# Keys stored by residue mod 4 for dilated attention, and each query part transposed once with the exchanged half copied by VectorE

## The chip, the cores and the metric

The kernel runs on one core of one Trainium2 chip. The metric is device time in microseconds (us) of one execution, as the median of the runs; smaller is better. The profile shows one execution of the same program, with its engines: TensorE (PE, and PEld for its weight loads), VectorE (DVE), ScalarE (ACT), GpSimd (POOL) and SyncE (SP). In this kernel SP issues all the DMA transfers.

## The reference

One inference step of one decoder layer, on a prompt of 2048 rows of 1024 numbers and on a sample of 8 x 8 tokens against a cache. A normed input goes through one input projection, whose columns are split among two mixers and their gates. The part that matters here is mixer A on the prompt: attention of 8 heads of width 64, in three branches, (window, dilation) = (128, 1), (512, 4) and (2048, 16), whose outputs are weighted by their softmax denominators.

```python
DILATED = ((128, 1), (512, 4), (2048, 16))

def mixer_layer(x, pos, attend, s0, ...):
    h = rmsnorm(x, norm_w)
    z = h @ w_in
    q, k, v, qb, kb, vb, g_lr, gate_a, gate_b = jnp.split(z, split_points(), axis=-1)
    q = rope(rmsnorm(heads(q, H_A), q_norm_w), pos)
    k = rope(rmsnorm(heads(k, H_A), k_norm_w), pos)
    o_a = attend(q, k, v)                       # mixer A
    o_b, s_fin = gla_chunked(qb, kb, vb, log_a, s0)   # mixer B, gated linear attention
    mixed = concatenate([o_a * silu(gate_a), rmsnorm(o_b, gla_norm_w) * silu(gate_b)])
    return x + mixed @ w_out, k, v, s_fin

def dilated_branch_prompt(q, k, v, window, dil):
    # rows are sorted by their residue mod dil; in each residue, blocks of 128 queries
    # see their own block of 128 keys and the one ahead of it
    qr, kk, vv = by_residue(q), with_prev(by_residue(k)), with_prev(by_residue(v))
    valid = (dist >= 0) & (dist < window // dil + 1) & (key_m >= 0)
    s = jnp.where(valid, einsum(qr, kk) * hd ** -0.5, -inf)
    m = s.max(-1); p = exp(s - m); den = p.sum(-1)
    return einsum(p, vv) / den, m + log(den)

def dilated_mixture(results):                   # over the three branches
    return einsum(softmax(lses), outs)
```

So branch 1 works on adjacent rows, branch 2 on rows 4 apart, branch 3 on rows 16 apart.

## The kernel before

Numbers go through TensorE in fp16, as a high part and a low part that together carry the fp32 value; a product of two such numbers is made of products of parts that are summed in PSUM.

**Projections.** `project` (L1052) multiplies tiles of 128 rows by one block of the input weights (v, q, k, then qkb, g, vb, gb), 24 products of 512 columns for a block of 512. `first(m)` runs v, q and k for the four tiles of group m (512 rows): at m=0 block by block, later tile by tile. Behind each, `qk_store` norms and rotates q and k, splits them into parts (ScalarE the high part, VectorE the low one) and stores them in device memory: `kp_d` holds for each row and head the key's high and low part (2 x 64), `qp_d` holds the query's high part twice and its low part twice (4 x 64). The values' parts go to `vp_d`.

**Keys and queries on chip.** A transposing DMA turns 128 rows by 128 columns into a block of 128 partitions by 128 columns. `keys(m, a)` does so for row tile a of group m, all 8 heads, into `kk`: partitions 0 to 63 hold the high part, 64 to 127 the low part, and the columns hold rows in their order, 512 for each of two groups. `queries(m, pp)` does the same for 4 heads (pp is the half of the heads) into `qq`, with 8 blocks: for each head one of (high, high) and one of (low, low). A score is then two products over 128 partitions, with a query block as weights and the keys as moving columns: high x (high, low), and low x (high, low).

**Attention.** `attend` works on 2 heads (branches 1 and 2) or 4 heads (branch 3), in three stages. `qk`: the score products (PE, L408); for each head one VectorE instruction that adds the mask and finds the maximum (L416), and one exponential on ScalarE (L419). `tr`: transposes of the result on PE (L426), which are split into parts (L388 to L393). `pv`: products with the values (L441); `added` (L452 to L458) then sums the two halves. `unit(m, pp, br, x)` makes two calls of attend, for branch 1 on block x of 128 queries of group m, for branch 2 on the queries of residue x mod 4. It loads its own value tile `v` (L825, for branch 2 by rows 4 apart) and stores its output to `o_d` (L840). In branch 2 both operands are read on chip in steps of 4 columns:

```python
qs = slice(x, 512, 4)
of = lambda k: k[:, :, qs] if nb == 2 else k[:, m % 2, qs]
```

With nb = 2 a block sees 256 keys, of two groups in branch 2; at m=0 branch 2 has one block of 128 keys. `kk` holds two groups; where the newer one stands in the first of the two places, the halves of keys, values and mask are in swapped order (`swap`).

`branch3(r)` handles residue r mod 16 for all 8 heads: transposing DMAs of 128 rows 16 apart (L879) give `T_q` (16 blocks, 512 KB) and `T_k` (8 blocks, 256 KB); a value tile; two calls of attend; a store of `o` (L896). The tiles `T_q`, `T_k`, `v` and `o` of branch 3 have two buffers each.

**What sets the order.** Calls of attend stand in a queue `work`. `pipeline()` runs item n's `qk`, item n-2's `pv` and item n-1's `tr` in turns, and runs an item's `pre` (transposes and value load) ahead of its `qk` and already behind the `qk` of the item before. `pump()` advances it a step at a time: during `first(m)` of group 1 on, 3 x 0.62 steps behind each group of three products, and later by `weave`, which mixes lists of work by their shares. A scheduler then places the instructions on each engine by a simulated timeline, and the engine works through its list in that order. DMAs are all in SP's list; beside what a transfer waits for by its data, it waits until the eighth transfer ahead of it on its semaphore ring has landed. The sample's score dots (`dot`: GpSimd L921, VectorE L922), loads of the cache and projections of mixer B run beside the attention.

Of the kernel before, what the change touches and what calls it, by code (L numbers as in the profile page):

```python
# [7 lines left out]
F32 = mybir.dt.float32  # L8
# [10 lines left out]
P = 128  # L19
# [33 lines left out]
def tile_hymba(ctx: ExitStack, tc: tile.TileContext, A: dict):  # L53
# [28 lines left out]
    qp_d = dram.tile([S, 4 * NH * HD], F16, name="qp_d")  # L82
# [23 lines left out]
    ident8 = cp.tile([P, P], F32, name="ident8")  # L106
    DVE.tensor_scalar(ident8[:], ident[:], 0.125, None, ALU.mult)

    ident64 = cp.tile([P, 64], F32, name="ident64")
    for r0 in (0, 64):  # L110
        DVE.tensor_copy(ident64[r0 : r0 + 64], ident8[r0 : r0 + 64, r0 : r0 + 64])
# [235 lines left out]
    with ExitStack() as c1:  # L347
# [18 lines left out]
        xp = right(c_first, "xp", 2)  # L366
        sp = c_att.enter_context(tc.tile_pool(name="sp", bufs=3))
# [376 lines left out]
        def qk_store(nm_, o, n, t, rows):  # L744
# [7 lines left out]
            c = 2 if nm_ == "q" else 1  # L752
            p_ = xp.tile([P, NH, 2, c, HD], F16, name=f"{nm_}p_{t}", tag=f"{nm_}p", bufs=1)
            src = o.rearrange("p (h d) -> p h d", h=NH)
            h, l = p_[:, :, 0], p_[:, :, 1]
            if c == 1:
                h, l = h[:, :, 0], l[:, :, 0]
                ACT.activation(h, src, AF.Copy, scale=scl["k"][:])
                DVE.scalar_tensor_tensor(l, src, scl["k"][:], h, ALU.mult, ALU.subtract)
            else:  # L760
                src = src.unsqueeze(2).to_broadcast([P, NH, 2, HD])
# [3 lines left out]
                (qp_d if c == 2 else kp_d)[rows, :], p_[:].rearrange("p h a c d -> p (h a c d)")  # L765
# [20 lines left out]
        def keys(m, a):  # L786

            r0 = 512 * m + P * a
            SP.dma_start_transpose(kk[:, :, m % 2, P * a : P * a + P], kp_d[r0 : r0 + P, :])

        def queries(m, pp):

            q = qs_[m, pp] = ap_.tile([P, 8, 512], F16, name=f"qq_{m}_{pp}", tag="qq")
            for a in range(4):
                r0 = 512 * m + P * a
                SP.dma_start_transpose(
                    q[:, :, P * a : P * a + P], qp_d[r0 : r0 + P, 1024 * pp : 1024 * pp + 1024]
                )

        def unit(m, pp, br, x):  # L800
            oc = slice(pp * 264, (pp + 1) * 264)
            if br == 1:
                n = 4 * m + x
                key, prev, dct, nb = n, n - 1, v1, (2 if n else 1)
                sel = lambda ap: ap[128 * n : 128 * n + 128]
            else:
                key, prev, dct, nb = (x, m), (x, m - 1), v2, (2 if m else 1)
                sel = lambda ap: ap[512 * m : 512 * m + 512].rearrange("(i c) f -> c i f", c=4)[x]
# [4 lines left out]
            def pre():  # L813
# [11 lines left out]
                SP.dma_start(vt[:], sel(vp_d[:, pp * 512 : (pp + 1) * 512]))  # L825
# [17 lines left out]
            for a in range(2):  # L843

                def scores(i, a=a):
                    if br == 2:
                        qs = slice(x, 512, 4)
                        of = lambda k: k[:, :, qs] if nb == 2 else k[:, m % 2, qs]
                    else:
                        qs = slice(P * x, P * x + P)  # L850
# [967 lines left out]
```

## Time and profile before

| | |
|---|---|
| runs (us) | 1457.05, 1461.98, 1464.38; median 1461.98 |
| profiled execution: span (us) | 1458.2 |
| mean granted TensorE clock over the span | 0.962 |
| instructions | 26397 |

The page gives for the profiled execution its span, from the first to the last instruction, and no separate time; the span lies 3.8 us under the median of the runs.

Where the stages lie, with the busy time of each engine in them (us, from the stretches of the trace):

| stretch (us) | what runs | PE | DVE | ACT | POOL | DMA share |
|---|---|---|---|---|---|---|
| 75 to 243 | v, q, k of the first groups, attention of m=0 | 141.17 of 168 | 120.60 | 104.64 | 60.01 | 0.69 |
| 243 to 655 | m=1 to 3, beside projections | 380.18 of 412 | 308.08 | 292.22 | 244.56 | 0.81 |
| 655 to 845 | branch 3 | 151.34 of 190 | 101.02 | 123.53 | 69.16 | 0.85 |
| 845 to 1458 | mixer B, gates, output, sample | 562.39 of 613 | 404.74 | 291.45 | 237.69 | 0.56 |

How to read the rows of the profile further down. A group's row has line, engine, operation, output<-inputs with partitions x elements, a count, and busy time with the mean of one in ns. A row of the timeline has start (us), length (us), engine, line, operation and a count of neighbours put together; SPq is the DMA queue's issue on SP. A row of DMA issues ends with the median time from issue to landing. A stretch's row has its length, the busy time of PE, PEld, DVE, ACT and POOL (with counts), the granted clock, the DMA share and GB/s. Busy time of an engine that nothing waits for costs nothing.

### The profile page before, as it was taken

What the parts mean: (1) busy time and instruction counts of PE and PEld (TensorE: products, weight loads), DVE (VectorE), ACT (ScalarE), POOL (GpSimd) and SP (SyncE); (2) the same over time, 40 slices, a digit from 0 to 9 for tenths busy, and PEclk for the clock granted to TensorE, in tenths of its full rate; (3) what the DMA queues carried; (4) which work ended last, traced back from release to release, by engine and by line L of the source; (5) the groups of instructions that cost most, each with busy time, mean ns of one, the idle gap of its engine ahead of it and who ended that gap; (6) DMA issues with size and microseconds to landing.
All of it is one profiled execution on the core that took longest, in us unless ns stands there. A gap on an engine that the chain in (4) does not pass through costs nothing.

```text
span 1458.2 us, 26397 instructions
## 1 busy us (share of the span) xinstructions
PE 1279.5 (88%) x8878; PEld 736.1 (50%) x8878; DVE 977.7 (67%) x2397; ACT 861.7 (59%) x2295; POOL 615.9 (42%) x564
## 2 busy tenths in 40 slices
PE   3787898989999889995869999889899969999997
PEld 1333455555555455664556655656655534444342
DVE  6576687788778946655655446799998697674222
ACT  7545687667668775765658744777787552222120
POOL 0042232656677644654351357555573345431000
PEclk9998999999999999997899999999999989999998
DMA  9867668577986799879998453333235759999661
GB/s 281 258 178 181 174 182 216 138 233 227 214 215 179 230 239 263 310 197 237 273 226 198 139 147 94 109 123 115 89 103 181 270 180 315 347 308 314 227 203 56
DMA packets 287962, 297.93 MB, mean 204 GB/s; under 512 B 158978, under 2 KB 189779, under 8 KB 287827
## 3 DMA queue, kind: packets, MB, share of 16 engines
q1 hardware_dynamic: 287826, 296.25, 69.6%
q8 instruction: 70, 1.15, 0.3%
q14 instruction: 66, 0.53, 0.1%
HBM read 183.19 MB, written 79.43 MB: 180 GB/s over the span
## 4 chain that ended last, share of the span: by engine, by line
PE 30%; DVE 20%; DMA 20%; ACT 12%; issue 7%; POOL 5%; SPq 5%; DVEq 0%; POOLq 0%; ACTq 0%
PE Y L1418 10%; DMA o_d<-o 5%; PE acc_gb L1052 4%; ACT p L419 3%; DMA k<-in_cache_k_win 3%; PE OS L1667 3%; DMA x<-in_x_prompt 2%; POOL pr L921 2%; DVE p L416 2%; PE s L408 2%; PE acc_qkb L1052 2%; DVE qbd L221 2%; PE t L426 1%; DVE sck L922 1%; PE acc_q L1052 1%
## 5 line engine op out<-in xcount | busy, mean ns | idle before, releaser
L1052 PEld LDWEIGHTS <-hr 128*128 128x128 f16 x1824 | 178.0, 100 | 149.7 <-issue 28.4
L921 POOL TENSOR_TENSOR pr<-k,qb 128x512 f32<-128x512 f32 x128 | 173.8, 1358 | 180.9 <-DVE sck L922 87.0
L419 ACT ACTIVATE p<-p,o 128x256 f32<-128x256 f32 (+1 forms) x384 | 173.0, 453 | 91.5 <-DVE o L416 84.6
L1052 PEld LDWEIGHTS <-hl 128*128 128x128 f16 x1248 | 122.9, 101 | 148.7 <-issue 33.6
L1418 PE MATMUL Y<-w_o,mh 128*128 128x512 f16 x768 | 180.9, 382 | 6.8 <-DVE xr L1425 4.4
L416 DVE CUSTOM_DVE_ANT_0 p<-s,m3w,scl_s 128x256 f32<-128x256 f32 (+1 forms) x384 | 143.7, 419 | 57.6 <-DMA o_d<-o 39.1
L393 POOL TENSOR_TENSOR pt<-p,pt 128x512 f16<-128x512 f32 (+1 forms) x80 | 94.8, 1186 | 158.0 <-ACT pt L392 121.8
L441 PE MATMUL O<-v,pt 128*128 128x128 f16 x1200 | 115.2, 223 | 33.6 <-POOL pt L393 15.3
L426 PE MATMUL t<-ident,p 128*128 128x128 f32 x600 | 116.2, 289 | 30.1 <-ACT p L419 26.8
L922 DVE TENSOR_REDUCE sck<-pr 128x8 f32<-128x512 f32 x128 | 87.0, 680 | 79.7 <-POOL pr L921 79.6
L1418 PEld LDWEIGHTS <-mh 128*128 128x128 f16 x768 | 72.0, 98 | 100.1 <-issue 27.0
L441 PEld LDWEIGHTS <-pt 128*128 128x128 f16 x1200 | 84.7, 100 | 68.3 <-POOL pt L393 21.5
L1052 PE MATMUL acc_v<-w_v,hl 128*128 128x512 f16 x384 | 99.8, 399 | 19.6 <-ACT zs_k L648 9.1
L408 PE MATMUL s<-kk,qq 128*128 128x256 f16 (+1 forms) x512 | 107.9, 324 | 9.6 <-DVE o L416 8.0
L1052 PE MATMUL acc_g<-w_g,hr 128*128 128x272 f16 (+1 forms) x768 | 103.9, 284 | 1.0 <-ACT vbs L722 1.0
L426 PEld LDWEIGHTS t<-ident,p 128*128 128x128 f32 x600 | 73.0, 146 | 58.4 <-ACT p L419 42.4
L1052 PE MATMUL acc_q<-w_q,hl 128*128 128x512 f16 x384 | 96.3, 388 | 1.6 <-ACT zs_q L648 1.4
L1052 PE MATMUL acc_k<-w_k,hl 128*128 128x512 f16 x384 | 95.1, 382 | 2.5 <-ACT zs_k L648 1.7
L1052 PE MATMUL acc_vb<-w_vb,hr 128*128 128x512 f16 x384 | 90.8, 384 | 5.8 <-DVE so_g L622 5.8
L1052 PE MATMUL acc_gb<-w_gb,hr 128*128 128x512 f16 x384 | 90.3, 391 | 5.8 <-DVE so_gb L622 5.8
L1384 ACT ACTIVATE mh<-tm 128x1024 f16<-128x1024 f16 x32 | 31.9, 1020 | 104.0 <-PE tm L1383 104.0
L210 ACT ACTIVATE E<-D_e 128x256 f32<-128x256 f32 (+1 forms) x168 | 67.9, 412 | 32.0 <-DVE ks L217 20.7
(523 smaller groups left out, 2590.8 us busy)
## 6 DMA issues: line engine op xcount, KB each, us to landing
k<-in_cache_k_win SPq DMA_DIRECT2D x104, 256.0 KB, 4.8
sv<-in_cache_v_win SPq DMA_DIRECT2D x104, 256.0 KB, 5.9
hr<-h_d SPq DMA_DIRECT2D x44, 512.0 KB, 4.7
qb<-q_d SPq DMA_DIRECT2D x64, 256.0 KB, 4.9
oc<-o_d SPq DMA_DIRECT2D x48, 264.0 KB, 5.7
o_d<-o SPq DMA_DIRECT2D x64, 132.0 KB, 4.1
x<-in_x_prompt SPq DMA_DIRECT2D x16, 512.0 KB, 5.6
h_d<-hl SPq DMA_DIRECT2D x16, 512.0 KB, 4.9
```

The costliest lines, as they stand in the source:

```text
L210: ACT.activation(E[rows, i, :n], D[rows, half], AF.Exp, scale=1.0 / 16.0)
L393: POOL.tensor_tensor(l, f, h, ALU.subtract)
L408: PE.matmul(s_ps[:, i * w : (i + 1) * w], q, k, start=(n == 0), stop=(n == len(prods) - 1),)
L416: DVE.tensor_tensor_reduce(s[:, sl], s_ps[:, sl], mask, neg, BIG, ALU.add, ALU.min, nmf(i))
L419: ACT.activation(s[:, sl], s[:, sl], AF.Exp, bias=nmf(i), scale=-1.0, accum_out=denf(i))
L426: PE.transpose(p_ps[:, i * P : (i + 1) * P], t["s"][:, i * P : (i + 1) * P], ident[:])
L441: PE.matmul(o_, t["pt"][:, c, (i * nb + b) * P : (i * nb + b + 1) * P], vf(i, b), start=(n == 0), stop=(n == 2 * nb - 1),)
L921: POOL.tensor_tensor(pr[:], kt, qt, ALU.mult)
L922: DVE.tensor_reduce(out, pr[:].rearrange("p (u k d) -> p u k d", u=2, k=4), AX.X, ALU.add)
L1052: PE.matmul(z, a_[:, k, :], w[:, p_, k, cols], start=(k == 0 and i == 0), stop=(k == KT - 1 and i == 2),)
L1418: PE.matmul(Y[:], a_[:, k, :], w_[:, part, k, :512], start=(i == 0), stop=(i == len(prods) - 1),)
L1667: PE.matmul(OS[32 * x : 32 * x + 32, 0:256], ps(x), vs_[bb][:, 256 * u : 256 * u + 256], start=(i == 0), stop=(i == 13),)
```

## The change

- **Keys.** `keys(m, c)` now transposes the 128 rows of group m with residue c mod 4, and `kk` has the form (head, residue, group mod 2, 128). Branch 2 reads the keys of a residue as adjacent columns, 128 or 256. Branch 1 reads the block x as four runs of 32 adjacent columns, one of each residue; its keys are then in another order, so its value tile is loaded with the same order of rows (`sel_k`), and it has a mask of its own, `m3c`, made from `m3w` by one GpSimd instruction.
- **Queries.** `qp_d` holds each part once. `queries` transposes 4 blocks of (high, low) in place of 8, and `exchanged` has VectorE copy them with the halves of the partitions swapped: (low, high). The two products of a score are then (high, low) x (high, low) and (low, high) x (high, low). Branch 2 still reads the queries in steps of 4. In branch 3 `T_q` is transposed with 8 blocks, and its other 8 are copied the same way.
- **The rest.** `ident8` is gone (ident64 is scaled straight from ident), and the two masks lie in a pool of their own.

```diff
@@ -79,7 +79,7 @@
     kp_d = dram.tile([S, 2 * NH * HD], F16, name="kp_d")
-    qp_d = dram.tile([S, 4 * NH * HD], F16, name="qp_d")
+    qp_d = dram.tile([S, 2 * NH * HD], F16, name="qp_d")
     vp_d = dram.tile([S, 2 * NH * HD], F16, name="vp_d")
@@ -103,12 +103,11 @@
     nw = const("nw", [P, KT], A["norm_w"][0].rearrange("(k p) -> p k", p=P))
-    ident8 = cp.tile([P, P], F32, name="ident8")
-    DVE.tensor_scalar(ident8[:], ident[:], 0.125, None, ALU.mult)
-
     ident64 = cp.tile([P, 64], F32, name="ident64")
     for r0 in (0, 64):
-        DVE.tensor_copy(ident64[r0 : r0 + 64], ident8[r0 : r0 + 64, r0 : r0 + 64])
+        DVE.tensor_scalar(
+            ident64[r0 : r0 + 64], ident[r0 : r0 + 64, r0 : r0 + 64], 0.125, None, ALU.mult
+        )
     ones = cp.tile([P, 1], F32, name="ones")
@@ -364,6 +363,7 @@
         xp = right(c_first, "xp", 2)
+        at1 = c_att.enter_context(tc.tile_pool(name="at1", bufs=1))
         sp = c_att.enter_context(tc.tile_pool(name="sp", bufs=3))
@@ -749,20 +749,17 @@
                 return
-            c = 2 if nm_ == "q" else 1
-            p_ = xp.tile([P, NH, 2, c, HD], F16, name=f"{nm_}p_{t}", tag=f"{nm_}p", bufs=1)
+            p_ = xp.tile([P, NH, 2, HD], F16, name=f"{nm_}p_{t}", tag=f"{nm_}p", bufs=1)
             src = o.rearrange("p (h d) -> p h d", h=NH)
             h, l = p_[:, :, 0], p_[:, :, 1]
-            if c == 1:
-                h, l = h[:, :, 0], l[:, :, 0]
+            if nm_ == "k":
                 ACT.activation(h, src, AF.Copy, scale=scl["k"][:])
...
             else:
-                src = src.unsqueeze(2).to_broadcast([P, NH, 2, HD])
                 ACT.activation(h, src, AF.Copy)
...
             SP.dma_start(
-                (qp_d if c == 2 else kp_d)[rows, :], p_[:].rearrange("p h a c d -> p (h a c d)")
+                (qp_d if nm_ == "q" else kp_d)[rows, :], p_[:].rearrange("p h a d -> p (h a d)")
             )
@@ -783,19 +780,28 @@
         qs_ = {}
-        def keys(m, a):
-
-            r0 = 512 * m + P * a
-            SP.dma_start_transpose(kk[:, :, m % 2, P * a : P * a + P], kp_d[r0 : r0 + P, :])
+        def by4(ap, r0, c):
+
+            return ap[r0 : r0 + 512].rearrange("(i c) f -> c i f", c=4)[c]
+
+        def keys(m, c):
+
+            SP.dma_start_transpose(kk[:, :, c, m % 2, :], by4(kp_d, 512 * m, c))
+
+        def exchanged(out, in_):
+
+            for j in range(2):
+                DVE.tensor_copy(out[64 * j : 64 * j + 64], in_[64 - 64 * j : 128 - 64 * j])
         def queries(m, pp):
-            q = qs_[m, pp] = ap_.tile([P, 8, 512], F16, name=f"qq_{m}_{pp}", tag="qq")
+            q = qs_[m, pp] = ap_.tile([P, 2, 4, 512], F16, name=f"qq_{m}_{pp}", tag="qq")
             for a in range(4):
...
                 SP.dma_start_transpose(
-                    q[:, :, P * a : P * a + P], qp_d[r0 : r0 + P, 1024 * pp : 1024 * pp + 1024]
-                )
+                    q[:, 0, :, P * a : P * a + P], qp_d[r0 : r0 + P, 512 * pp : 512 * pp + 512]
+                )
+            exchanged(*(q[:, a].rearrange("p h c -> p (h c)") for a in (1, 0)))
         def unit(m, pp, br, x):
@@ -803,9 +809,10 @@
                 sel = lambda ap: ap[128 * n : 128 * n + 128]
+                sel_k = lambda ap: sel(ap).rearrange("(j c) f -> c j f", c=4)
             else:
                 key, prev, dct, nb = (x, m), (x, m - 1), v2, (2 if m else 1)
-                sel = lambda ap: ap[512 * m : 512 * m + 512].rearrange("(i c) f -> c i f", c=4)[x]
+                sel = sel_k = lambda ap: by4(ap, 512 * m, x)
             swap = nb == 2 and m % 2 == 0 and (br == 2 or x == 0)
@@ -822,7 +829,7 @@
                 )
-                SP.dma_start(vt[:], sel(vp_d[:, pp * 512 : (pp + 1) * 512]))
+                SP.dma_start(vt[:], sel_k(vp_d[:, pp * 512 : (pp + 1) * 512]))
                 dct[(pp, key)] = vt
@@ -843,24 +850,21 @@
                 def scores(i, a=a):
+                    k = kk[:, 4 * pp + 2 * a + i]
                     if br == 2:
+                        k = k[:, x] if nb == 2 else k[:, x, m % 2]
                         qs = slice(x, 512, 4)
-                        of = lambda k: k[:, :, qs] if nb == 2 else k[:, m % 2, qs]
                     else:
+                        k = k.rearrange("p c s (y j) -> p (s y) c j", j=32)
+                        y1 = 4 * (m % 2) + x + 1
+                        k = k[:, 0::7] if swap else k[:, y1 - nb : y1]
                         qs = slice(P * x, P * x + P)
-                        if x or nb == 1:
-                            of = lambda k: k[:, m % 2, P * (x - nb + 1) : P * (x + 1)]
-                        elif m % 2:
-                            of = lambda k: k.rearrange("p s c -> p (s c)")[:, 384:640]
-                        else:
-                            of = lambda k: k.rearrange("p s (b c) -> p (s b) c", c=P)[:, 0::7]
-                    k = of(kk[:, 4 * pp + 2 * a + i])
                     q = qs_[m, pp]
-                    return [(q[:, 2 * (2 * a + i) + part, qs], k) for part in range(2)]
+                    return [(q[:, part, 2 * a + i, qs], k) for part in range(2)]
                 out.append(attend(
                     f"{br}_{m}_{pp}_{x}_{a}", 2, nb, scores,
-                    masks12[swap][:, 256 - nb * P :],
+                    masks12[br][swap][:, 256 - nb * P :],
                     lambda i, b, a=a: T["v"][b][:, (2 * a + i) * P : (2 * a + i + 1) * P],
@@ -876,8 +880,11 @@
                     t = b3.tile([P, nb, P], F16, name=f"T3_{nm_}_{r}", tag=f"T{nm_}")
-                    SP.dma_start_transpose(t[:], by16(src, r))
+                    SP.dma_start_transpose(t[:, 0:8], by16(src, r))
                     T[nm_] = t
+                exchanged(
+                    *(T["q"][:, a : a + 8].rearrange("p h i -> p (h i)") for a in (8, 0))
+                )
                 yield
@@ -899,7 +906,7 @@
                     lambda i, a=a: [
-                        (T["q"][:, 2 * (2 * i + a) + part], T["k"][:, 2 * i + a])
+                        (T["q"][:, 8 * part + 2 * i + a], T["k"][:, 2 * i + a])
                         for part in range(2)
@@ -955,10 +962,16 @@
         gnw = const1("gnw", [P, P], A["gla_norm_w"].to_broadcast([P, P]))
-        m3w = const1("m3w", [P, 384], A["c_m3"])
+        m3w = at1.tile([P, 384], F32, name="m3w")
+        SP.dma_start(m3w[:], A["c_m3"])
+        m3c = at1.tile([P, 384], F32, name="m3c")
+        POOL.tensor_scalar(
+            m3c[:].rearrange("p (b c j) -> p b c j", c=4, j=32),
+            m3w[:].rearrange("p (b j c) -> p b c j", c=4, j=32), 1e-10, None, ALU.mult,
+        )
         DVE.tensor_scalar(m3w[:], m3w[:], 1e-10, None, ALU.mult)
-        masks12 = (m3w[:, 0:256], m3w[:, 128:384])
+        masks12 = {n_: (m[:, 0:256], m[:, 128:384]) for n_, m in ((1, m3c), (2, m3w))}
         m3 = m3w[:, 128:256]
@@ -990,7 +1003,7 @@
         DVE.reciprocal(unq[:], scl["q"][:])
-        kk = ap_.tile([P, NH, 2, 512], F16, name="kk", tag="kk", bufs=1)
+        kk = ap_.tile([P, NH, 4, 2, P], F16, name="kk", tag="kk", bufs=1)
         from collections import deque
```

The order on SP around the first transposes of keys of group 0. Names end in a number of the tile: `kp_1076` and `kp_1154` are the keys' parts of row tiles 2 and 3, `hl` the transposed input of a later tile, `x` an input tile. Before:

```order
L764 DMA kp_d<-kp_1076 128x1024
L503 DMA h_d<-hl_1004 128x2048
L727 DMA out_v_win_prompt<-vs_1266 128x512
L789 DMA_TRANSPOSE kk<-kp_d 128x8x128
L736 DMA vp_d<-vp_1269 128x1024
L643 DMA cs_q_2047<-in_c_rope 128x128
L746 DMA out_k_win_prompt<-t_k_1147 128x512
L499 DMA_TRANSPOSE hl_1082<-ht_1096 128x16x128
L764 DMA kp_d<-kp_1154 128x1024
```

and after:

```order
L761 DMA kp_d<-kp_1079 128x1024
L503 DMA h_d<-hl_1007 128x2048
L727 DMA out_v_win_prompt<-vs_1271 128x512
L736 DMA vp_d<-vp_1274 128x1024
L643 DMA cs_q_2054<-in_c_rope 128x128
L499 DMA_TRANSPOSE hl_1085<-ht_1099 128x16x128
L746 DMA out_k_win_prompt<-t_k_1150 128x512
L472 DMA x_1161<-in_x_prompt 128x1024
L761 DMA kp_d<-kp_1157 128x1024
L503 DMA h_d<-hl_1085 128x2048
L789 DMA_TRANSPOSE kk<-kp_d 128x8x128 x4
L499 DMA_TRANSPOSE hl_1163<-ht_1177 128x16x128
```

Before, each transpose of keys stands a few rows behind the store of its own row tile; now all four stand together behind the store of the fourth. On PE 414 products of projections stand ahead of the first score product, 323 before.

The order on VectorE in branch 3, around the first mask (`L416`) of residue 6 (`p_6_0`); `T_q_8751` is the query tile of residue 8, `so_g` a tile of the projection of g, `sck` a sum of the sample's dots. Before:

```order
L416 ISA p_5_1_8466,o_5_8379<-s_5_1_8465,m3w,scl_s 128x128
L416 ISA o_5_8379 128x1
L922 TENSOR_REDUCE sck_7867<-pr_7_4_7976 128x2x4
L622 TENSOR_SCALAR so_g_9903<-acc_g_0_9878,wi_g 128x256
L416 ISA p_6_0_8534,o_6_8492<-s_6_0_8533,m3w,scl_s 128x128
```

and after:

```order
L622 TENSOR_SCALAR so_g_9955<-acc_g_0_9930,wi_g 128x256
L929 TENSOR_REDUCE sck_7888<-pr_7_2_8318 128x2x4
L458 TENSOR_TENSOR o_4_8275<-O_4_1_8584,ol_8596 128x4x64
L389 SCALAR_TENSOR_TENSOR pt_5_0_8558<-t_5_0_8541,pt_5_0_8558 128x512
L929 TENSOR_REDUCE sck_7888<-pr_7_2_8321 128x2x4
L630 ISA so_g_9955,gmax_a<-so_g_9955,sa_g_9957 128x256
L630 ISA gmax_a 128x1
L794 COPY T_q_8751<-T_q_8751 64x1024 x2
L416 ISA p_6_0_8567,o_6_8525<-s_6_0_8566,m3w,scl_s 128x128
```

The two copies for residue 8 now stand between the work for residue 5 and the first mask of residue 6.

## The prediction

> **What bounds the kernel now.** I read the page's busy shares and slices first, then stretches cut at the attention's groups, then the chain of waits.
>
> ```profile
> PE 1279.5 (88%) x8878; PEld 736.1 (50%) x8878; DVE 977.7 (67%) x2397; ACT 861.7 (59%) x2295; POOL 615.9 (42%) x564
> PE   3787898989999889995869999889899969999997
> DMA  9867668577986799879998453333235759999661
> ```
>
> TensorE is nearest to full, and the DMA engines are full in places. The change touches roughly 75 to 840 us (slices 3 to 23), so I cut that. Columns: length, busy time of each engine with its count, granted clock, DMA share.
>
> ```profile
> 312.00:344.00 32.00, 27.79 (x211) 17.77 (x210) 28.01 (x64) 22.56 (x64) 18.79 (x16) 1.00 0.76 217
> 415.00:448.00 33.00, 32.67 (x216) 19.89 (x214) 27.67 (x67) 23.31 (x64) 24.56 (x18) 1.00 0.64 202
> 617.00:643.00 26.00, 26.00 (x182) 16.24 (x181) 14.78 (x44) 16.16 (x46) 14.34 (x12) 1.00 0.64 187
> 655.00:845.00 190.00, 151.34 (x1247) 108.49 (x1246) 101.02 (x390) 123.53 (x425) 69.16 (x68) 0.91 0.85 214
> ```
>
> The first is a group of branch 1 (8 calls of attend), the next two are groups of branch 2, the last holds the 16 residues of branch 3. In branch 2 TensorE is full (32.67 of 33, 26.00 of 26). In branch 1 it has room, while VectorE stands at 28 of 32. In branch 3 no engine is full, and the chain there reads:
>
> ```profile
> 664.41 1.19 SPq L879
> ...
> 696.38 1.50 SPq L879
> ...
> 708.64 2.33 SPq L879
> ...
> 723.55 2.79 SPq L879
> ...
> 739.76 6.15 DMA o_d<-o
> 746.07 0.35 DVE p L416
> ```
>
> A store of `o` must land before `L416` may reuse that buffer (two buffers), and the store queues on SP behind transposes of `L879`. That wait, from the instructions of `L416` between 655 and 840 us, is
>
> ```profile
>   DMA o_d<-o: 22.7, 9
> ```
>
> so 22.7 us in nine waits.
>
> **The change, part by part.** *Keys read adjacent.* Four products on 256 columns, branch 1 and then branch 2; then on 128 columns at m=0, again 1 then 2 (start, length, count):
>
> ```profile
> 257.12 0.60 PE L408 MATMUL s<-kk,qq 128*128 128x256 f16 x4
> 305.30 1.07 PE L408 MATMUL s<-kk,qq 128*128 128x256 f16 x4
> 190.37 0.39 PE L408 MATMUL s<-kk,qq 128*128 128x128 f16 x4
> 214.31 0.63 PE L408 MATMUL s<-kk,qq 128*128 128x128 f16 x4
> ```
>
> Branch 2 loses 0.47 us per four on 256 columns and 0.24 on 128. The loss doubles with the moving columns while the weight load always has 128, so it belongs to the moving side, the keys, which the change makes adjacent; the queries keep their step of 4 as weights. Branch 2 has 6 groups with m over 0, each with 8 calls of four products: 48 x 0.47 = 22.6 us at most. Should the weight load with its step still set the pace, four products take what the 128-column row of branch 2 shows, 0.63, and the gain is 48 x 0.44 = 21 us. I take 21. The 16 fours at m=0 give 0 to 3.8 us; nearest is a load that still binds, so 0. Of the 21 us, full TensorE returns all (the two full groups, 7 us), and the other four, where TensorE is 83 to 93% busy, half (7 us): **-14**, ends 0 and -26.
>
> The Trainium skill ("SBUF — State Buffer", "A bandwidth-pool intuition that's wrong", the note on cachelines under Door 1) says that two hits in a 16-byte line give full bandwidth, so that 8 bf16 may be stepped for free. By it a step of 4 fp16 cost nothing, this term would be 0 and the sum below 14 us higher. The two rows on 256 columns contradict it, so the rows decide.
>
> In branch 1 the keys are now runs of 32 adjacent columns; the nearest rows are those above (0.60 whole, 1.07 single), and runs of 64 bytes are nearer the whole: 0, upper end 60 x 0.47 = 28 us.
>
> *First attention later.* A unit's keys now come from all four row tiles. In time, before (the last row is us to landing):
>
> ```profile
> 108.33 0.53 SPq L764 DMA_DIRECT2D kp_d<-kp  x1
> ...
> 123.03 0.44 PE L408 MATMUL s<-kk,qq 128*128 128x128 f16 x5
> ...
> 142.76 1.17 SPq L764 DMA_DIRECT2D kp_d<-kp  x1
> ...
> 256.67 0.61 PE L426 MATMUL t<-ident,p 128*128 128x128 f32 x4
> ...
> 306.20 0.63 PE L441 MATMUL O<-v,pt 128*128 128x128 f16 x8
> ...
> kk<-kp_d SPq DMA_TRANSPOSE x16, 4.5
> ```
>
> The first scores ran at 123 us; the fourth store of keys went out at 143, and with some 3 us to land, four transposes on SP and 4.5 us of landing they would start near 155. Projections fill TensorE meanwhile, in the new order 91 more products ahead of the first score. What they can't fill is attention done early, eight calls of scores, four transposes and eight value products: 8 x (0.5 + 0.61 + 0.63) = 14 us at most. TensorE was not full there (the first slices), and VectorE and ScalarE serve the projections faster without attention, so I take a little under a third: **+4**, ends 0 and +14. For m above 0 three of the four transposes can go while the fourth residue of the group ahead is still read, and I cost them 0.
>
> *Queries stored once.*
>
> ```profile
> L763 DVE TENSOR_TENSOR qp<-t_qk,qp 128x1024 f16<-128x1024 f32 x12 | 16.3, 1357 | 0.2 <-ACT qp L762 0.2
> L759 DVE SCALAR_TENSOR_TENSOR kp<-t_qk,scl_k,kp 128x512 f16<-128x512 f32 x12 | 13.8, 1151 | 0.0
> L505 DVE TENSOR_SCALAR x_s<-x_s,rs 64x1024 f32<-64x1024 f32 x1 | 0.7, 745 | 0.0
> L123 DVE TENSOR_SCALAR rv_qk<-qs_q 128x16 f32<-128x16 f32 x12 | 13.5, 1122 | 0.3
> L123 DVE TENSOR_SCALAR rv_x<-ss 128x1 f32<-128x1 f32 x16 | 2.4, 148 | 17.6 <-ACT jk L487 17.6
> ```
>
> Splitting a query tile halves (1.36 to some 0.7 us) 16 times: VectorE -10, ScalarE about -7 us, both beside TensorE. The copies are new: 16 of 64x2048 and 32 of 64x1024 fp16. `L505` moves the same 4 KB a partition in 0.745 us; half of it I put at 0.45. That is 12 + 14 = 26 us. The upper end is one element a step, as `L763` runs (1.36 us per 1024): 43 + 43 us. And the 16-column `L123`, whose work is 0.15 us, took 1.12 us just where GpSimd works on the same rows: single-source ops can wait for GpSimd some 1 us, so I add 0.5 for a pair. For branches 1 and 2 the net is 16 x 0.75 + 8 x 0.5 - 10 = +6 us on a VectorE that is 57 to 88% busy, half of it on the path: **+3**, ends -5 and +15.
>
> *Transposes.*
>
> ```profile
> L796 SPq DMA_TRANSPOSE qq<-qp_d x32: 1237/1302/2987, 83.4 to 538.1; - x32
> L879 SPq DMA_TRANSPOSE T_q<-qp_d x16: 1902/3584/5968, 543.5 to 795.9; - x16
> L879 SPq DMA_TRANSPOSE T_k<-kp_d x16: 1245/1392/2257, 555.1 to 800.9; - x16
> T_q<-qp_d SPq DMA_TRANSPOSE x16, 5.8
> T_k<-kp_d SPq DMA_TRANSPOSE x16, 4.5
> o_d<-o SPq DMA_DIRECT2D x16, 264.0 KB, 3.7
> DMA packets 287962, 297.93 MB, mean 204 GB/s; under 512 B 158978, under 2 KB 189779, under 8 KB 287827
> ```
>
> (The first three: min/median/max ns on SP. The next three: us to landing.) `T_q` becomes as large as `T_k`: SP is freed 16 x (3.58 - 1.39) = 35 us, and landing shortens by 1.3 us. Only what stands in the chain counts: 1.2 + 1.5 + 2.3 + 2.8 = 7.8 us of `L879` between 655 and 845, of which 60% goes, -5, and of the 22.7 us of store waits a sixth, -4. Against it stand the copies: the DVE order puts the copy for residue r+2 ahead of `L416` of residue r, so that `L416` now waits for the store and for the transpose plus 2 x 0.45 us. Transpose (4.5) and store (3.7, issued behind it) land within 1 us of each other, so I put +0.3 us on each of 14 residues: +4. Branch 3: **-5**, ends -20 and +20. Bytes of `qq`, of `T_q` and of the stores of queries halve (12.6 MB of 298); what of this falls in branches 1 and 2 is hidden behind TensorE, 0, lower end -8.
>
> The second mask (one GpSimd pass early on), the dropped identity and the strided rows of `kk` (`T_k` reads rows 16 apart in the same 4.5 us) are 0: nothing waits for them before 123 us.
>
> Sum: 1458.2 - 14 + 4 + 3 - 5 = 1446 us of span. The three runs have a median of 1462.0, 3.8 above this span, so 1450 for the median.
>
> **Rivals.** *A: nothing to measure (1460).* VectorE takes over: groups of branch 1, without the slow reads, last as long (32 us) as those of branch 2 (33), at 28 us of VectorE. Then TensorE's 21 us turn into waiting but for 4, and with the other terms 2 us are left of the gain. Against it: TensorE at 26.00 of 26 with VectorE at 14.8.
>
> *B: slower by copies (1480).* In branch 3 the copy stands ahead of `L416` in an engine that works in order. Were `T_q` to land as late as now (5.8 us) with each copy held up as the 16-column `L123` is, `L416` starts some 2.4 us later than the store allows, for each residue: 14 x 2.4 = 34 in place of the +4 above, 30 us more than the forecast. It decides once copies end more than 2.2 us (what SP gains per transpose) behind the store. For it: the DMA share of 0.85 there. Against it: half the bytes.
>
> *C: slower by the loads of values (1471).* Branch 1 loads its 32 value tiles with rows taken 4 apart in four runs. If such a load ran on four of 16 DMA engines, its 128 KB, 0.64 us at the page's mean of 204 GB/s, would take 2.6: on those four +1.9 us x 32 = 62 us in branches 1 and 2, at a DMA share of 0.64 to 0.76 (the stretches above); a third of it on the path is +21, and 1471.
>
> ```profile
> v<-vp_d SPq DMA_DIRECT2D x64, 128.0 KB, 4.4
> ```
>
> For it no row speaks: that is the landing today. The Trainium skill ("DMA: Bandwidth & Descriptors", "Why a DMA increments its semaphore by 16 and not by 1") has the engine count divide the slowest dimension of both patterns, which here would be 4; no row of this trace has such a load.
>
> *D: faster still (1429).* Branch 3 frees up with SP: all 7.8 us of `L879` and half of the 22.7 us go, the copies hide (-19 in place of -5), and TensorE returns all 21.
>
> **How the numbers follow.** Forecast 0.46 (1436 to 1456 by itself), A 0.20, B 0.12, C 0.08, D 0.14. Half a per cent, 7 us, is what a measurement of this kernel can tell. Faster is D and nearly all of the forecast: 0.57. No change is A with the forecast's edge: 0.21. Slower is B, C and a little of A: 0.22. The range reaches over C to 1474 and over D to 1424 and leaves out most of B and the far side of D.
>
> **What would show it.** Four scores of branch 2 in 0.60 to 0.66 us; first scores near 155 us; copies of 0.75 and 0.45 us (1 us more if GpSimd holds them); `T_q` on SP at 1.4 us; `L416` still waiting mainly for `o_d<-o`. Wrong if `L416` waits for the copies, if branch 2's groups stay at 33 us, or if the values' loads land at 6 us and more.

## The result: slower by 1.4%, outside the range

The changed kernel took 1479.05 us (median of four runs, 1474.15 to 1485.74), the kernel before 1459.51 (four runs beside them): a ratio of 1.0136, 95% interval [1.0094, 1.0178]. 1450 was forecast, with a range to 1474.

The page of the changed kernel begins so (busy us with share; TensorE, its clock and the DMA engines in 40 slices):

```profile
span 1481.8 us, 26480 instructions
PE 1272.1 (86%) x8878; PEld 738.0 (50%) x8878; DVE 1007.6 (68%) x2444; ACT 855.7 (58%) x2295; POOL 623.7 (42%) x565
PE   3884997888888778887689999898988979989997
PEclk9897999999999989999799999999999989999999
DMA  9765665678756599878877553343234569998662
```

TensorE is busy 7 us less than before (1279.5), on a span 24 us longer: it stands idle 210 us, not 179. The single steps came out nearly as forecast. First the group of scores in the kernel before, then groups and rows of the changed kernel (line, engine, operation, count, busy and mean, idle time ahead; or min/median/max in ns; or start and length; or who waited for what: us, times, longest):

```profile
L408 PE MATMUL s<-kk,qq 128*128 128x256 f16 (+1 forms) x512 | 107.9, 324 | 9.6 <-DVE o L416 8.0
L408 PE MATMUL s<-kk,qq 128*128 128x256 f16 (+1 forms) x512 | 81.6, 277 | 26.4 <-DVE o L416 25.1 <-issue 1.3
308.72 1.04 PE L408 MATMUL s<-kk,qq 128*128 128x256 f16 x8
159.14 0.61 PE L408 MATMUL s<-kk,qq 128*128 128x128 f16 x8
L794 DVE COPY T_q<-T_q x32: 420/422/1284, 528.3 to 823.8; 64x1024 f16<-64x1024 f16 x32
L794 DVE COPY qq<-qq x16: 686/690/1657, 105.9 to 568.4; 64x2048 f16<-64x2048 f16 x16
L883 SPq DMA_TRANSPOSE T_q<-qp_d x16: 1231/1261/2882, 522.5 to 819.4; - x16
DVE p L416 <- DMA o_d<-o: 29.8, 17, 6.0
DVE T_q L794 <- DMA T_q<-qp_d: 29.6, 12, 7.2
```

The scores of branches 1 and 2 are 26 us shorter (81.6 for 107.9). Eight products of branch 2 now take 1.04 us. The first scores come at 159 us, the copies take 0.42 and 0.69 us and the transposes of `T_q` hold SP 1.26 us, all at the median. Two rows speak otherwise: TensorE waits 25.1 us for `L416` to free a score buffer (8.0 before), and the copies wait 29.6 us for `T_q`, with `L416` behind them in VectorE's list.

To see where the time went, I cut both traces where the same number of TensorE products had started (600, 1900, 3400 and 4500 of 8878). Length, busy time of PE, PEld, DVE, ACT and POOL, clock, DMA share, GB/s; first before, then after:

```profile
0.00:176.00 176.00, 124.40 (x601) 59.16 (x602) 110.95 (x262) 102.87 (x236) 38.50 (x47) 0.93 0.77 216
176.00:390.00 214.00, 197.47 (x1302) 117.53 (x1301) 173.38 (x421) 156.19 (x443) 110.57 (x85) 0.98 0.73 196
390.00:633.80 243.80, 222.68 (x1503) 134.34 (x1500) 174.70 (x434) 173.18 (x474) 147.16 (x110) 0.98 0.84 238
633.80:806.00 172.20, 134.57 (x1102) 94.78 (x1101) 98.24 (x369) 111.23 (x380) 65.80 (x54) 0.90 0.93 232
```
```profile
0.00:185.10 185.10, 131.24 (x601) 60.08 (x602) 117.56 (x262) 101.31 (x231) 47.47 (x51) 0.91 0.70 203
185.10:399.70 214.60, 185.35 (x1302) 114.83 (x1301) 172.52 (x431) 153.08 (x445) 113.38 (x88) 0.96 0.70 188
399.70:662.20 262.50, 220.39 (x1501) 135.95 (x1501) 186.55 (x447) 169.73 (x470) 146.03 (x113) 0.94 0.76 209
662.20:826.20 164.00, 133.66 (x1101) 95.69 (x1100) 108.53 (x397) 114.43 (x391) 56.97 (x46) 0.90 0.78 198
```

The start costs 9 us, the second stretch nothing, the third (groups 2 and 3) 19, branch 3 gives 8 back, and the rest adds 3. In the third stretch TensorE starts as many products and is idle 42 us, 21 before. The waits behind this, in that stretch, before and then after:

```profile
PE s L408 <- DVE o L416: 4.3, 4, 2.7
DVE p L416 <- DMA o_d<-o: 7.3, 4, 2.5
```
```profile
PE s L408 <- DVE o L416: 16.9, 9, 6.2
DVE p L416 <- DMA o_d<-o: 11.3, 5, 6.0
```

Of the 21 us more some 14 stand ahead of scores (18.2 for 4.6) and 6 ahead of the products with the values (17.4 for 11.4). TensorE's busy time fell by only 2 us there, although the scores of the stretch fell from 52.7 to 40.9: the granted clock was 0.94 in place of 0.98. By an estimate from these rows the other 170 us would take 170 x 0.98 / 0.94 = 177, and 179.5 were taken. What lowered the clock, no run shows.

One wait shows how the idle time comes about (rows of SP, VectorE, ScalarE and TensorE):

```profile
514.68 3.80 SPq L554 DMA_DIRECT2D wr_g<-in_w_in  x6
518.58 0.42 SPq L847 DMA_DIRECT2D o_d<-o  x1
525.02 0.48 DVE L416 CUSTOM_DVE_ANT_0 p<-s,m3w,scl_s 128x256 f32<-128x256 f32 x1 [5.97 <-DMA o_d<-o]
525.60 0.51 ACT L419 ACTIVATE p<-p,o 128x256 f32<-128x256 f32 x1 [6.29 <-DVE o L416]
525.97 1.01 PE L408 MATMUL s<-kk,qq 128*128 128x256 f16 x4 [6.20 <-DVE o L416]
```

A store of `o`, whose data VectorE had written by 514.1 us, stands in SP's list behind six loads of weights. `L416` can't reuse the buffer until the store lands at 524.9, and three engines stand still for 6 us. The diff doesn't touch these loads or this store: what can differ is their place in the list.

### The profile page after: what moved, and what is told of

Its sections match the earlier page's. It is cut to its first block, busy times and chain, and to the rows that moved or that the text cites. A ratio compares the mean times of both kernels' runs of the same rounds, so it can differ in the third digit from the quotient of the medians.

```text
span 1481.8 us, 26480 instructions
## 1 busy us (share of the span) xinstructions
PE 1272.1 (86%) x8878; PEld 738.0 (50%) x8878; DVE 1007.6 (68%) x2444; ACT 855.7 (58%) x2295; POOL 623.7 (42%) x565
## 4 chain that ended last, share of the span: by engine, by line
PE 26%; DVE 26%; DMA 25%; ACT 11%; issue 6%; POOL 3%; SPq 3%; DVEq 0%; POOLq 0%; ACTq 0%
PE Y L1431 7%; DMA qb<-q_d 4%; DMA o_d<-o 4%; PE acc_vb L1065 3%; PE OS L1680 3%; DVE p L416 3%; ACT p L419 2%; DMA T_q<-qp_d 2%; PE acc_g L1065 2%; DMA x<-in_x_prompt 2%; DMA k<-in_cache_k_win 2%; POOL pr L928 2%; DVE qbd L220 1%; DVE sck L929 1%; ACT E L209 1%
## 5 line engine op out<-in xcount | busy, mean ns | idle before, releaser
L441 PE MATMUL O<-v,pt 128*128 128x128 f16 x1200 | 119.0, 225 | 48.5 <-POOL pt L393 18.1
L426 PE MATMUL t<-ident,p 128*128 128x128 f32 x600 | 121.1, 296 | 18.1 <-ACT p L419 16.2
L1065 PE MATMUL acc_v<-w_v,hl 128*128 128x512 f16 x384 | 96.6, 400 | 25.6 <-ACT zs_q L648 11.0
L416 DVE CUSTOM_DVE_ANT_0 p<-s,m3w,scl_s 128x128 f32<-128x128 f32 (+1 forms) x256 | 88.6, 395 | 30.3 <-DMA o_d<-o 26.5
L408 PE MATMUL s<-kk,qq 128*128 128x256 f16 (+1 forms) x512 | 81.6, 277 | 26.4 <-DVE o L416 25.1
L1065 PE MATMUL acc_vb<-w_vb,hr 128*128 128x512 f16 x384 | 94.1, 392 | 2.8 <-DVE so_g L622 2.8
L1065 PE MATMUL acc_k<-w_k,hl 128*128 128x512 f16 x384 | 92.0, 383 | 3.9 <-ACT zs_k L648 3.4
```

The source lines that it names most:

```text
L408: PE.matmul(s_ps[:, i * w : (i + 1) * w], q, k, start=(n == 0), stop=(n == len(prods) - 1),)
L416: DVE.tensor_tensor_reduce(s[:, sl], s_ps[:, sl], mask, neg, BIG, ALU.add, ALU.min, nmf(i))
L426: PE.transpose(p_ps[:, i * P : (i + 1) * P], t["s"][:, i * P : (i + 1) * P], ident[:])
L441: PE.matmul(o_, t["pt"][:, c, (i * nb + b) * P : (i * nb + b + 1) * P], vf(i, b), start=(n == 0), stop=(n == 2 * nb - 1),)
L1065: PE.matmul(z, a_[:, k, :], w[:, p_, k, cols], start=(k == 0 and i == 0), stop=(k == KT - 1 and i == 2),)
```

## The experiments

Theories at the start. W: the products are faster, but the late start and VectorE's fixed line keep the gain. B: the copies cost the time. C: branch 1's value loads, rows 4 apart in four runs, are slow. Later O: the scheduler's order for this kernel is an unlucky one; I, its rival: slow loads and copies cost it together, in any order. Each median (of 6 to 12 runs) stands beside its ratio to the kernel before on the same chip (1460.5 to 1462.9 us).

**Parts of the change (e1 to e4).** e1 and e2 are the change with one half taken back; e3 drops the calls of `exchanged` and reads one block for both products; e4 loads adjacent rows:

```diff
-                SP.dma_start(vt[:], sel_k(vp_d[:, pp * 512 : (pp + 1) * 512]))
+                SP.dma_start(vt[:], sel(vp_d[:, pp * 512 : (pp + 1) * 512]))
```

> The keys' part alone: kk by residue, branch 1 with runs of 32 keys, permuted value rows and a mask of its own; queries doubled in device memory as before, no copies. Before is 1460, the whole change 1479. Theory W (the products get faster, but attention starts some 17 us later and VectorE, in order, hands the masks out no faster, so the keys' part brings the loss): 1468 to 1480. Theory B (the copies cost the time): 1442 to 1452, by the 14 to 21 us of the scores less some 4 for the start. Theory C (value loads of branch 1 slow): 1465 to 1475 with products of the values waiting for v.

> The queries' part alone: each part stored once, half the transposes, exchanged halves copied by VectorE; keys, values and masks as before. Theory W: 1452 to 1464 (about no change; branch 3 some 8 us shorter, as in the whole change, the copies of branches 1 and 2 costing about as much). Theory B: 1475 to 1485. Theory C: no effect of its own, 1455 to 1460.

> The whole change without the 48 copies: both products of a score read the one transposed block, so the second one multiplies other numbers than it should (scores are wrong by that part). Theory W: 1468 to 1476, the copies cost 3 to 10 us of the 20 lost. Theory B: 1445 to 1458, the loss is gone. Theory C: 1470 to 1479.

> The whole change with branch 1's value tiles loaded as 128 adjacent rows instead of four runs of rows 4 apart; their rows then don't stand in the order of the keys, so branch 1's outputs are mixed wrongly. Theory C: 1455 to 1463. Theories W and B: 1476 to 1482, as the whole change.

| kernel | us | ratio, interval |
|---|---|---|
| e1 keys only | 1470.4 | 1.0063 [1.0039, 1.0088] |
| e2 queries only | 1446.8 | 0.9912 [0.9881, 0.9942] |
| e3 no copies | 1443.1 | 0.9876 [0.985, 0.9901] |
| e4 adjacent value rows | 1452.5 | 0.9936 [0.9915, 0.9957] |

In these orders the loss sits with the keys' half, and the queries' half is a gain. But e3 gains 36 us and e4 27, more together than was lost: the parts don't add. And e2, e3 and e4 came out 2 to 5 us under every range that a theory gave them.

**The loads by themselves (e5 to e8).** e5 puts the four-run loads into the kernel before (`sel_k` for branch 1). e6 is e3 and e4 together. e7 and e8 keep the keys by residue, but let the mask instruction read the scores from PSUM in the order of the rows, so that the value tiles can be loaded as adjacent rows and the second mask is not needed (`i_` are the scores of branch 1):

```diff
+                        i_ = i_.rearrange("p (c y) -> p y c", c=4)
+                    DVE.tensor_tensor_reduce(o_, i_, m_, neg, BIG, ALU.add, ALU.min, nmf(i))
...
+                        k = k.rearrange("p c s (y j) -> p c (s y) j", j=32)
```

> The kernel before with one thing of the change: branch 1's 32 value tiles loaded as four runs of rows 4 apart (their order then doesn't fit the keys, so branch 1's outputs are mixed wrongly). Theory C (such a load runs on four of the 16 DMA engines and comes late): 1470 to 1485, and 32 x 11 = 352 fewer completion events of DMAs than before. Theory W (the loads are harmless, the order of the instructions made the difference between the whole change and its form with adjacent rows): 1456 to 1466.

> The whole change without the 48 copies (both products read the one transposed block) and with branch 1's value tiles loaded as 128 adjacent rows (mixed wrongly). Without copies alone it was 1443, with adjacent rows alone 1452, the whole 1479. If the copies and the slow loads cost time apart from each other: 1479 - 36 - 27 = 1416. If they cost it together (the copies wait in VectorE's order for transposes that stand behind the slow loads): 1435 to 1445.

> The whole change with branch 1's keys read by residue, but the mask instruction reads the scores of branch 1 from PSUM in the order of the rows (steps of 64 or 32 elements), so that value tiles are 128 adjacent rows and the second mask is gone. Theory C: 1446 to 1456, as with adjacent rows alone. If the stepped read of PSUM costs VectorE time (0.48 us an instruction becoming 0.9, 152 of them): 1465 to 1480.

> The keys' part alone (queries doubled, no copies), with branch 1's masks reading the scores in the order of the rows and value tiles of 128 adjacent rows. Keys alone with four-run loads was 1470, before 1461. Theory C: 1446 to 1456. Theory W (the keys' part brings the loss by its late start and by VectorE's order): 1464 to 1472.

| kernel | us | ratio, interval |
|---|---|---|
| e5 before, four-run loads | 1466.2 | 1.0038 [1.0019, 1.0057] |
| e6 no copies, adjacent rows | 1433.5 | 0.9817 [0.9791, 0.9843] |
| e7 whole, rows in order | 1448.8 | 0.9925 [0.9902, 0.9949] |
| e8 keys only, rows in order | 1462.5 | 1.0019 [0.9998, 1.0039] |

The instruction lists tell which pairs are clean. e5 has the same rows in the same order as before on TensorE and VectorE, and so has e6 against e3 (four and five rows of SP move). These two pairs price the loads alone: 0.4% and 0.6%, 5 to 9 us, each known to some 0.2 to 0.4%. Between e4 and the whole change, though, a quarter of TensorE's and VectorE's rows stand elsewhere, and there the difference is 27 us. e6, at 1433.5, is far from the 1416 that the two parts would give if they added. e7 came out where theory C put it, but e8, at 1462.5, in no range that was given: with the slow loads gone, the keys' half still gains nothing.

**The order (e9, e10, e13 to e17).** e9 asks for `T_k` ahead of `T_q` in branch 3; the others move one number, which says how fast attention is advanced beside the projections:

```diff
-            rate = 0.62
+            rate = 0.64
```

> The whole change, with one line moved: branch 3 asks for T_k ahead of T_q. From the middle of the attention on the scheduler then makes another order (2000 of 7957 TensorE rows and 600 of 2446 on VectorE move); the work is the same. Theory O (of the 27 us between the whole change, 1479, and its form with adjacent value rows, 1452, only the 5 to 10 us that the loads cost in kernels of one order belong to the loads, the rest to an unlucky order): 1455 to 1475. Theory I (copies that wait in VectorE's line for transposes behind the slow loads make the loads dear, whatever the order): 1474 to 1485.

> The whole change with the rate at which attention is advanced beside the projections at 0.64 in place of 0.62: an order that differs from the first group's attention on (3000 of 7957 TensorE rows). Theory O: 1455 to 1475. Theory I: 1474 to 1485.

> The kernel before with the rate at 0.60 in place of 0.62: the same work in another order (2600 of 7957 TensorE rows move). If orders differ for this kernel as they did for the whole change (1454 to 1479): anywhere from 1455 to 1485, and 1461 would be a lucky one if both other rates come out slower. If before is insensitive: 1456 to 1466.

> The kernel before with the rate at 0.64: another order (3500 of 7957 TensorE rows move). The same two expectations: 1455 to 1485 if orders matter here as much as for the whole change, 1456 to 1466 if not.

> The whole change with the rate at 0.60. Theory O (1479 is the unlucky end of its orders): 1455 to 1472. Theory I (the copies and the slow loads cost it whatever the order, and 0.64 is the lucky one): 1474 to 1485.

> The whole change with branch 1's masks reading the scores in the order of the rows (value tiles of 128 adjacent rows), rate 0.64. It was 1449 at 0.62. If the four-run loads cost 5 to 10 us in any order, it is that much under the whole change at 0.64 (1454): 1443 to 1449. If the order decides: 1440 to 1465.

> The form with adjacent value rows (masks read in the order of the rows), rate 0.60. It was 1449 at 0.62 and 1450 at 0.64; the whole change 1473, 1479 and 1454. If the four-run loads are what makes the whole change dear and sensitive to its order: 1446 to 1456. If only orders differ: 1455 to 1475.

| rate | before | whole change | whole, rows in order (e7's form) |
|---|---|---|---|
| 0.60 | 1468.4 (1.0053) | 1473.5 (1.0087) | 1470.6 (1.0060) |
| 0.62 | 1 | 1479.1 (1.0136) | 1448.8 (0.9925) |
| 0.64 | 1464.0 (1.0021) | 1453.7 (0.9951) | 1450.1 (0.9925) |

The intervals of these ratios are 0.2 to 0.4% to either side; e9 took 1467.9 (1.0058). The same work takes 1454 or 1479 us, by a rate that changes only the order. The third stretch of e10, cut as above, and the two waits in it:

```profile
397.00:638.20 241.20, 212.16 (x1502) 133.92 (x1501) 182.90 (x455) 170.58 (x477) 147.36 (x112) 0.95 0.80 224
PE s L408 <- DVE o L416: 7.3, 5, 2.6
DVE p L416 <- DMA o_d<-o: 3.8, 1, 3.8
```

In the changed kernel the two waits were 16.9 and 11.3 us. 21 of the 28 us between the two spans (1481.8 and 1453.3) lie in this stretch; up to it the two traces run within 3 us of each other. 13 of the 21 are idle time of TensorE (42 us against 29), with fewer and shorter waits of `L416` for stores and of TensorE for `L416`. The other 8 are busy time, with a clock of 0.94 against 0.95.

So O holds in the main: the change doesn't lose 1.4% whatever the order. e9 lies in O's range, e10 just under it, e15 (1473.5) between the ranges of O and of I. In e16 and e17 the expectation that only orders differ came true, and the one that the loads decide did not: rows in order did not keep that form out of the bad orders. The rates move the time by 25 and 22 us for the two changed forms and by 7 for the kernel before. Whether the change makes the kernel more sensitive to its order, three orders each don't settle.

The granted clock mostly goes with the time: over their runs its mean is 0.944 and 0.945 in e18 (below) and e15, 0.963 and 0.961 in e2 and e6, and 0.954 to 0.955 in the kernel before; e10, fast with 0.951, doesn't fit. TensorE is busy some 1270 us, so a hundredth of the clock is some 13 us by estimate. Whether an order is slow because its clock is low, or the other way round, no run tells.

**Two terms of the prediction alone (e11, e12).** e11 lets branch 2 of the kernel before read adjacent columns (`slice(128 * x, 128 * x + 128)` in place of step 4). e12 puts branch 2 ahead of branch 1 at m=0.

> The kernel before, but branch 2 reads 128 adjacent columns of kk for each group instead of every fourth (other keys than it should, so branch 2's outputs are wrong): the faster products without a later start, copies, permuted loads or a second mask. TensorE gives all of the 21 us: 1440. The forecast's term: 1447 plus or minus 3. Rival A (VectorE, and TensorE's clock that halves after idle spells, take it): 1455 to 1463.

> The kernel before, with branch 2 ahead of branch 1 in the first group alone, so that its first attention needs the keys of all four row tiles and starts some 20 us later, as in the change. The forecast's term for the late start: +4, 1463 to 1468. If the lag that the trace after shows from the start on (17 us of attention) is paid in full: 1472 to 1480.

e11 took 1460.7 us (1.0014 [0.9988, 1.004]): no gain, though its products are as much shorter as in the change. Its page, its group of scores and that of its products with the values:

```profile
span 1457.7 us, 26370 instructions
PE 1269.4 (87%) x8878; PEld 736.7 (51%) x8878; DVE 982.6 (67%) x2397; ACT 858.8 (59%) x2295; POOL 622.4 (43%) x564
L408 PE MATMUL s<-kk,qq 128*128 128x256 f16 (+1 forms) x512 | 81.6, 272 | 10.9 <-DVE o L416 10.0 <-DMA kk<-kp_d 0.9
L441 PE MATMUL O<-v,pt 128*128 128x128 f16 x1200 | 117.9, 225 | 41.7 <-POOL pt L393 16.7 <-ACT pt L388 6.6 <-ACT pt L392 6.3
```

Of the 26.3 us that the scores lost, TensorE's busy time fell by 10.1 alone: its other work took 16 us more. Its idle time grew by 9.6 us, and the span fell by 0.5. Ahead of the products with the values it waits 41.7 us, 33.6 before, for the split of the exponentials (`pt`) above all; its waits for `L416`, branch 3 included, grew from 10.6 to 14.3. The mean granted clock of this execution is 0.956, and 0.962 in the trace before; but over all runs on that chip it is 0.954 for e11 and 0.955 for the kernel before, so the clock doesn't explain why e11 gains nothing.

The stretches of e11, cut as above, from the second on, and the rest:

```profile
175.00:390.30 215.30, 190.52 (x1301) 114.11 (x1300) 174.69 (x424) 156.56 (x445) 111.57 (x86) 0.98 0.76 200
390.30:629.10 238.80, 213.69 (x1501) 134.12 (x1500) 180.56 (x436) 171.23 (x474) 146.79 (x112) 0.96 0.86 240
629.10:799.50 170.40, 134.90 (x1103) 97.00 (x1100) 95.96 (x363) 110.83 (x381) 62.59 (x52) 0.87 0.94 230
799.50:1457.70 658.20, 603.37 (x4378) 332.42 (x4378) 419.59 (x915) 317.31 (x766) 263.07 (x269) 0.97 0.56 183
```

In the second stretch TensorE is 7 us less busy and the stretch is 1 us longer; in the third it is 9 us less busy, and 5 us come back. The rest, 652 us before, is 6 us longer, though the scores that were changed lie ahead of it. Over all the traces of this case it takes 644 to 658 us, so this part alone can hide a gain of that size. (A fifth of TensorE's rows also stand elsewhere in e11.)

e12 took 1465.3 (1.0030 [1.0011, 1.0049]), +4.4 us. A third of TensorE's rows stand elsewhere in it. In its trace the scores start at 154 us, the first stretch is 9 us longer than before, as in the change, the second 9 shorter and the rest 5 longer.

**Copies on ScalarE (e18).** e7 with `ACT.activation(..., AF.Copy)` in `exchanged`:

> The form with adjacent value rows at 0.62, with the 48 copies of exchanged halves on ScalarE instead of VectorE. Leaving the copies out gained 19 us (1452 to 1434), with VectorE in the way of the masks. If VectorE's line is the price: 1436 to 1446. If the copies' time or their wait for the transposes is the price on any engine (ScalarE makes the exponentials): 1448 to 1460.

1476.6 us (1.0111 [1.0078, 1.0145]).

```profile
L797 ACT ACTIVATE T_q<-T_q 64x1024 f16<-64x1024 f16 x32 | 33.8, 1055 | 18.5 <-DMA T_q<-qp_d 18.2
L797 ACT ACTIVATE qq<-qq 64x2048 f16<-64x2048 f16 x16 | 30.5, 1909 | 5.7 <-DMA qq<-qp_d 5.5
```

ScalarE needs 64 us for them where VectorE needed 30 in e7, in front of its exponentials, and waits 24 us for the transposes where VectorE waited 28. By busy time VectorE is the better place. The time lies over both expected ranges. This is one order more, with four tenths of TensorE's rows elsewhere, so the 28 us to e7 can't be put down to the copies alone.

## Why the prediction was wrong

The forecast was 1450, with a range to 1474; 1479 was measured. One term failed by its mechanism (the keys), one was put at nothing (the value loads), and one was missing (the order).

- *Keys adjacent, -14.* This is the step that failed: "full TensorE returns all" of the 7 us in the two full groups, and the other groups half. The products are shorter, even by a little more than reckoned (26 us for 21; 0.52 us per four), but e11 gives +2 us [-2, +6] in place of -14. In its trace 16 us less of TensorE's work in the two stretches with 256 columns gave 4 us back. A group at 32.67 of 33 says that TensorE was busy, not that the other engines hand over work faster: with shorter products it stood before the next wait, for `pt` and for `L416`. This is rival A's mechanism, with the whole chain of an attention in VectorE's place; A got 0.20. e8, which has the keys' half without the slow loads, gains nothing either, in another order. The Trainium skill's rule that such steps are free ("SBUF — State Buffer", the note on cachelines under "Door 1: The DMA port swizzle") is contradicted again: with the reads of branch 2 alone changed, the mean product fell from 324 to 272 ns.
- *First attention later, +4.* The time was right (159 us for 155). The price isn't settled: the first stretch is 9 us longer in the change and in e12, and that e12 as a whole measured +4.4 is in part luck, since its second stretch gave the 9 back and its rest took 5.
- *Copies, and the halved split, +3.* The durations were right at the median (0.69 and 0.42 for 0.75 and 0.45), with some held up: 34 us in all, where 26 and half a us a pair for being held up were reckoned. Their price on the path isn't settled: leaving them out gained 19 us (e4 to e6) and 36 (the whole change to e3), in other orders each time.
- *Branch 3, -5.* The stretch is 8 us shorter. That `L416` stays with the store was half right: 29.6 us of waiting moved to the copies, which the prediction had named as a sign of being wrong. Rival B put 30 us more there for such waits; with the stretch shorter, the loss isn't B's.
- *Queries as a whole* (copies and branch 3, -2 by the sum) measured -13 in e2, in one order. Its trace is 16 us shorter: 12 lie in branch 3 (159.8 us) and 8 in the rest (644.3 us), which the queries don't touch, while the second stretch is 8 longer.
- *Value loads, left at nothing; rival C (1471, 0.08)* was true in kind and too dear in size. Each such load leaves 5 completion records where any other leaves 16 (17762 in all, 18114 before: 32 x 11 fewer); the first comes 1.0 us after issue and the last at a median of 4.5 us, where the other value loads take 4.1. By the records' times a load lands 0.4 us later than the others here (0.6 and 0.8 in e1 and e5), not the 1.9 that was reckoned, and all 32 cost 5 to 9 us. The Trainium skill ("DMA: Bandwidth & Descriptors", "Why a DMA increments its semaphore by 16 and not by 1") says that engines in use post one each and the issuing sequencer writes the rest at once: four and one are the 5 seen here.
- *What the sum lacked* is a price for the order itself. It took one order's waits and corrected them part by part, and the range held only the parts. The runs show 25 us between orders of the same work for the change, 7 for before, 22 for e7's form.

What stays open: the change's own worth. Over the three rates, means of the ratios are 1.0025 for before, 1.0058 for the change and 0.9970 for e7's form. With a spread of half a per cent and more in each column, three orders don't tell the first two apart, and hint at best that the third is faster. That the loss of 1.4% belongs to the order in good part is shown by e10; how much of the rest is loads or copies is argued. As kernels to run, each in its one order, e2 (1446.8) and e7 (1448.8) beat both the kernel before and the changed one.

## What to carry to other kernels

In a kernel whose order a scheduler makes, a change of layout is also a new draw of the order: turn a harmless knob for both versions (here a rate) and compare several draws before a per cent is put down to the change. That an engine is busy doesn't yet say that the time of a shortened instruction comes back: look at what the engine will wait for next, and test the gain by itself with other data. Cut the traces also where the change has no part: what moves there isn't the work that was changed. Loads in four runs of rows cost this kernel 5 to 9 us here, and reading the scores in another order cost nothing: reorder where an engine reads, if it can be had.

## What the hardware showed that was not expected

A mask instruction that reads 256 scores from PSUM in steps of 64 elements took as long as one that reads them in line (medians of 0.477 and 0.478 us in e7, over 120 and 96 instructions), so reordering there was free. Over all masks of e7, 256 and 128 columns together, the median is 0.471 us, and 0.470 before:

```profile
L421 DVE CUSTOM_DVE_ANT_0 p<-s,m3w,scl_s x384: 332/471/485, 155.7 to 812.6; 128x256 f32<-128x256 f32 x108, 128x128 f32<-128x128 f32 x84
```

ScalarE moves 64x2048 fp16 from one half of the partitions to the other in 1.91 us (e18), VectorE in 0.69 (the changed kernel).
